# Moving the large operands of TensorE from 64 past a multiple of 512 bytes to a multiple of 512 bytes

## The chip, the core and the metric

The kernel runs on one core of one Trainium2 chip. The metric is the device time of one execution in microseconds (us); lower is better. The engines are named as the profile names them: PE is TensorE's matmul, PEld its weight load, DVE is VectorE, ACT is ScalarE, POOL is GpSimd, and SP (SyncE) issues nearly all DMAs. Each core has an on-chip memory, SBUF, of 128 partitions; an address below means a byte offset within a partition, the same in all 128. The change is about where in it tiles start. "Residue" stands for a start address modulo 512 bytes.

## The reference, cut to what matters

One decoder layer over 2048 tokens of width 1024, in float32: a gated DeltaNet mixer with 8 heads of 128, a cross-attention to 256 memory rows with 4 heads, an output projection with residual and layer norm, and a squared-ReLU MLP of width 4096 with residual and layer norm.

```python
proj = x @ w_in                                   # q, k, v, z of 8 heads, gates, memory queries
qkv = silu(causal_depthwise_conv(qkv, conv_w))    # width 4
q, k = l2_normalize(q), l2_normalize(k)
o = chunk_gated_delta_rule(q, k, v, g, beta)      # per chunk a triangular inverse, then a state update
o = rms_norm(o, gate_norm_w) * silu(z)
m = memory_attention(mq, mem_k, mem_v)
x = layer_norm(ALPHA * x + concat([o, m]) @ w_out, ln1_g, ln1_b)
x = layer_norm(ALPHA * x + square(relu(x @ w_ff1)) @ w_ff2, ln2_g, ln2_b)
```

## The kernel before

The 2048 tokens go in four blocks of 512 (`for b in range(NB)`, line 1111). Each block runs the same stages: the input projections and the DeltaNet heads, the memory attention, the output projection, and the MLP.

**Precision by threes.** A large float32 product is made of three matmuls of the type fp32r: each operand is split into a high part (a cast on ACT) and a low part (a subtraction on DVE) by `split` (line 450), and `mm3` (line 468) issues high by high, high by low and low by high. Weights arrive by DMA in `wraw` tiles and are split into `whl` tiles, 1024 columns of high and 1024 of low. The activations of the block lie in `Thi` and `Tlo`. For one block this makes 36 column groups of `w_in` times 8 times 3 = 864 such matmuls, 288 for the output projection, 768 for the first MLP product and 672 for the second: 2592 a block and 10368 in all, 512 columns wide but for some of the first MLP product, which are done in two halves of 256. The second MLP product (`ff_seven`, line 991) is a seven-product scheme; its stationary operands are the tiles `xh` and `xl`, and two of the high ones lie in the tile `kq0` under the name `hq`.

**The heads.** `dense(t)` (line 673) projects q, k, v and z of head t. For q, k and v, ACT copies the result into a `raw` tile with three halo columns ahead of it, and DVE adds the four taps from it into `cq`, `ck`, `cv`. q and k are then split into the tiles `kq0` and `kq1`. PE transposes k and then q into one PSUM bank (`ptk`, then `ptq`; the bank is `ga0` or `ga1` by the parity of the head). From the transposed k, ACT makes four squares with a running sum (`jk`: the square itself goes to a scrap tile `jk`, only the sum in `ss` is used) and four scaled copies `kd`; from the transposed q four squares `jq`. POOL turns the sums into `rk` and `bh`. `gdn_a(t)` (line 818) multiplies k by k and q (`pkq`), scales by `bh` into `dl`, inverts the triangular matrix (`invert`, beginning with the copies `Lq`), and transposes v (`ptv`). `gdn_b(t)` (line 869) walks four chunks in order (`R`, `vt`, the state), makes four squares of the result with their sums (`joss` is the scrap tile), normalizes, transposes and writes the head's output `cat`. The loop at line 1127 calls, for step t, `gdn_b(t-2)`, `gdn_a(t-1)` and `dense(t)`, in this order. The memory attention comes in the last steps; the output projection is then taken in three parts (line 1176): heads 0 to 3, the memory heads, heads 4 to 7.

**The planner.** None of this is issued in program order. Every instruction is recorded by the class `Recorder`, and its method `issue` (line 220) lays them out by list scheduling with estimated durations: an instruction earlier in the program goes first among those that are ready. A tile has a tag with a number of buffers. `place` and `ahead` (lines 237 to 259) give the buffers of a tag out strictly in program order of the tiles' first uses: with one buffer, the next tile of the tag can be taken only when every earlier tile of that tag has had it and given it back. `jk`, `jq` and `joss` are three tags (the tag is the tile's name, line 387) with one buffer each. The planner's costs depend on shapes alone, not on addresses. The engines then run the instructions in the planned order.

**Where tiles lie.** Pools lie one behind the other in the order of lines 369 to 375, each tile rounded up to 32 bytes. By the sizes in the code, `cst` ends at residue 64, so `wraw`, `whl` (pool `wp`), the 4 KB token tiles, `Thi` and `Tlo` (pool `tp`) start at residue 64. The two `raw` tiles of 515 floats take 2080 bytes each, 4160 together, so `kq0` and `kq1` behind them lie at residue 128. The 112 floats of the pool `pad` (line 372) bring the pool `sp`, with `xh`, `xl`, `ch`, `cl` and the head's tiles, back to residue 64.

Of the kernel before, what the change touches and what calls it, by code (L numbers as in the profile page):

```python
# [8 lines left out]
F32 = mybir.dt.float32  # L9
# [5 lines left out]
P = 128  # L15
TB = 512
# [320 lines left out]
def hybrid_layer(  # L337
# [24 lines left out]
    nc = tc.nc  # L362
# [6 lines left out]
    cst = ctx.enter_context(tc.tile_pool(name="cst", bufs=1))  # L369
    wp = ctx.enter_context(tc.tile_pool(name="wp", bufs=1))  # L370
    tp = ctx.enter_context(tc.tile_pool(name="tp", bufs=1))
    pad = ctx.enter_context(tc.tile_pool(name="pad", bufs=1))
    nc.vector.memset(pad.tile([P, 112], F32, name="shift"), 0.0)
    sp = ctx.enter_context(tc.tile_pool(name="sp", bufs=1))
    sm = ctx.enter_context(tc.tile_pool(name="sm", bufs=1))
    ps = ctx.enter_context(tc.tile_pool(name="ps", bufs=1, space=bass.MemoryType.PSUM))
# [6 lines left out]
    def slot(name, tag="s0", dt=F32, shape=(P, TB)):  # L383
        return rec.buf(sp, shape, dt, tag, BUFS[tag], name)

    def small(name, shape, bufs=3, dt=F32):
        return rec.buf(sm, shape, dt, name, bufs, name)

    def bank(name, tag):
        return rec.buf(ps, (P, TB), F32, tag, PBUFS[tag], name)  # L390
# [2 lines left out]
        return ap.rearrange("p (c f) -> p c f", c=NC)  # L393


    ident = cst.tile([P, P], F32, name="ident")
    make_identity(nc, ident)
    ones = cst.tile([P, P], F32, name="ones")
# [31 lines left out]
    rec = Recorder(nc, tc)  # L430
    BN_DIM = nc.vector.BN_STATS_DIM
    nc = rec
# [17 lines left out]
    def split(src, hi, lo, eng=None):  # L450
        nc.scalar.copy(out=hi, in_=src)
        (eng or nc.vector).tensor_tensor(out=lo, in0=src, in1=hi.bitcast(F32), op=ALU.subtract)
# [28 lines left out]
    def load_in(b, u):  # L481

        if b == 0:
            rt = rec.buf(wp, (P, 1024), F32, "wraw", NR, "wraw")
            nc.sync.dma_start(out=rt, in_=w_in[u])
            t, hi, lo = hilo(rt)
            nc.sync.dma_start(out=wsc[u], in_=t.bitcast(F32))
        else:
            t, hi, lo = pair()
            nc.sync.dma_start(out=t.bitcast(F32), in_=wsc[u])  # L490
        return as_cols(hi, lo)
# [33 lines left out]
    def tok_tile(name):  # L525
        return rec.buf(tp, (P, D), F32, "tok", 8, name)
# [14 lines left out]
    def project(o, w, T, n=TB, t0=0):  # L541
        for k in range(KT):
            kk = [100 * k + t for t in range(t0 // P, (t0 + n) // P)]
            mm3(o, w[0][k], w[1][k], T[0][:, k, t0:t0 + n].part(*kk), T[1][:, k, t0:t0 + n].part(*kk),
                k == 0, k == KT - 1)
# [127 lines left out]
    def dense(b, h, T, G, w0=None):  # L673
        res = {}
        for nm, o in (("q", QO), ("k", KO), ("v", VO), ("z", ZO)):
            w = w0 if w0 and nm == "q" else load_in(b, o // P + h)
            a = bank("a" + nm, "acc")
            project(a, w, T)
            c = slot("c" + nm, "d")
            th = slot("th", "th")  # L680
            if nm == "z":
                nc.scalar.activation(th, a, AF.Tanh, scale=0.5)
                nc.vector.scalar_tensor_tensor(out=c, in0=th, scalar=1.0, in1=a, op0=ALU.add, op1=ALU.mult)
            else:
                gi = o // P + h
                raw = rec.buf(tp, (P, TB + 3), F32, "raw", 2, "raw")
                nc.scalar.copy(out=raw[:, 3:], in_=a)
                nc.gpsimd.tensor_copy(raw[:, 0:3], halo[:, gi].part(gi))
                if b < NB - 1:
                    nc.gpsimd.tensor_copy(halo[:, gi].part(gi), raw[:, TB:TB + 3])  # L690
                nc.scalar.activation(c, a, AF.Copy, scale=cw[:, 72 + gi:73 + gi])
                for j in range(3):
                    nc.vector.scalar_tensor_tensor(out=c, in0=raw[:, j:j + TB], scalar=cw[:, j * 24 + gi:j * 24 + gi + 1],
                                                   in1=c, op0=ALU.mult, op1=ALU.add)
                nc.scalar.activation(th, c, AF.Tanh, scale=0.5)
                nc.vector.scalar_tensor_tensor(out=c, in0=th, scalar=1.0, in1=c, op0=ALU.add, op1=ALU.mult)
            res[nm] = c
            if nm in "qk":
                if "kq" not in res:
                    res["kq"] = [rec.buf(tp, (P, 2, TB), F32R, "kq%d" % u, 1, "kq") for u in range(2)]  # L700
                i = "kq".index(nm)
                split(c, res["kq"][0][:, i].part(i), res["kq"][1][:, i].part(i), KQE)
        par = "ga%d" % (h % 2)
        ss = small("ss", [P, 2 * NC])
        kd = res["kd"] = slot("kd", "s%d" % (h % 2))
        for n, nm in enumerate("kq"):
            pt = bank("pt" + nm, par)
            for c in range(NC):
                nc.tensor.transpose(pt[:, c * P:(c + 1) * P], res[nm][:, c * P:(c + 1) * P], ident)
            for c in range(NC):  # L710
                j = small("j" + nm, [P, P], 1)
                nc.scalar.activation(j, pt[:, c * P:(c + 1) * P], AF.Square,
                                     accum_out=ss[:, n * NC + c:n * NC + c + 1])
            if nm == "k":
                for c in range(NC):
                    nc.scalar.activation(kd[:, c * P:(c + 1) * P], pt[:, c * P:(c + 1) * P], AF.Copy,
                                         scale=G["ekd"][:, h, c:c + 1])
        nc.gpsimd.tensor_scalar_add(ss, ss, 4 * RMS_EPS)
        rk = small("rk", [P, NC])
        nc.gpsimd.tensor_tensor(out=rk, in0=ss[:, :NC], in1=mhalf, op=ALU.pow)  # L720
        res["e4"] = small("e4", [P, NC], 4)
        nc.gpsimd.tensor_scalar_mul(res["e4"], ss[:, NC:], P * RMS_EPS)
        res["vbs"] = small("vbs", [P, NC])
        nc.gpsimd.tensor_tensor(out=res["vbs"], in0=G["betah"][:, h], in1=rk, op=ALU.mult)
        bh = res["bh"] = small("bh", [P, NC])
        nc.gpsimd.tensor_tensor(out=bh, in0=G["beta"][:, h], in1=rk, op=ALU.mult)
        nc.gpsimd.tensor_tensor(out=bh, in0=bh, in1=rk, op=ALU.mult)
        res["nbe"] = small("nbe", [P, NC], 4)
        nc.gpsimd.tensor_tensor(out=res["nbe"], in0=bh, in1=G["neg"][:, h], op=ALU.mult)
        return res  # L730

    def invert(L, par):
# [14 lines left out]
        nc.vector.tensor_copy(Xc, i16.unsqueeze(2).to_broadcast([P, 16, NC]))  # L747
        B = small("Bc", [P, 16, NC], 2)
        for j in range(15):
            w = j + 1  # L750
            nc.vector.stream_shuffle(B[:, :w], Xc[:, :w], [j] * 16 + [16 + j] * 16)
            nc.vector.tensor_tensor(out=B[:, :w], in0=B[:, :w],
                                    in1=Lc[:, j:j + 1].to_broadcast([P, w, NC]), op=ALU.mult)
            nc.vector.tensor_tensor(out=Xc[:, :w], in0=Xc[:, :w], in1=B[:, :w], op=ALU.subtract)
        Z = small("Z32", [P, NC, 32], 2)
# [54 lines left out]
    def sumsq(p3, nm):  # L810
        o = small(nm, [P, NC])
        for c in range(NC):
            j = small("j" + nm, [P, P], 1)
            nc.scalar.activation(j, p3[:, c], AF.Square, accum_out=o[:, c:c + 1])
        return o

# [52 lines left out]
    def gdn_b(h, A, G, cat):  # L869
# [5 lines left out]
        for c in range(NC):  # L875
# [11 lines left out]
            nc.vector.scalar_tensor_tensor(out=Sh, in0=Sh, scalar=sc("el", c), in1=pc[:, 2 * P:3 * P],  # L887
                                           op0=ALU.mult, op1=ALU.add)
        oss = sumsq(po, "oss")
        m4 = small("m4", [P, NC])  # L890
        nc.gpsimd.tensor_scalar_mul(m4, oss, 1.0 / P)
# [79 lines left out]
    def keep_sums(u, j):  # L971

        if j == 0:
            B = [t[:, n * TB:(n + 1) * TB].part(n) for t in (tok_tile("wq"), tok_tile("wq")) for n in range(2)]
        else:
            B = [rec.buf(tp, (P, TB + 3), F32, "raw", 2, "wq")[:, :TB] for _ in range(2)]
            kq = rec.buf(tp, (P, 2, TB), F32, "kq1", 1, "wq")
            B += [kq[:, n].part(n) for n in range(2)]
        for n in range(4):
            nc.sync.dma_start(out=B[n], in_=w_ff2[u + 2 * (n // 2), n % 2][:, j * TB:(j + 1) * TB])  # L980
        for i, o, x, y in ((1, 0, 1, 0), (3, 1, 3, 1), (2, 3, 3, 0), (4, 2, 2, 3)):
            nc.vector.tensor_tensor(out=B[o], in0=B[x], in1=B[y], op=ALU.subtract)
            nc.sync.dma_start(out=tsc[u, i][:, j * TB:(j + 1) * TB].part(j), in_=B[o])
# [7 lines left out]
    def ff_seven(b, ff1_tiles, relu2, add, norm2):  # L991
        Q = 2 * P
        for g in range(NS):
# [3 lines left out]
            for v in range(2):  # L997
# [6 lines left out]
                for part in ((0, 1, 2, 3),) if g == 0 and v == 0 else ((0,), (1,), (2,), (3,)):  # L1004
                    if b == 0:
                        for j in range(2):
                            if 2 * j in part:
                                keep_sums(u0 + v, j)
# [260 lines left out]
```

## Time and profile before

| what | us |
|---|---|
| median of 3 runs (2996.95 to 2998.56) | 2997.76 |
| the profiled execution, its own time | 2999.08 |
| its span, first to last instruction | 2997.4 |

The profile is a page for one execution and a trace of it that can be asked for views: groups of instructions, waits, the chain of work that ended last, a timeline, and the busy time in given stretches. A row of the timeline gives the start in us, the duration in us, engine, line, operation, output and inputs by the program's names, shape, and a count where equal instructions follow each other. All recorded operations have line 320, that of the recorder's helper, so they are told apart by their tiles. A matmul's duration includes a modelled tail that overlaps the next one; the step from one start to the next is what PE's time is made of. A float32 matmul (not fp32r) shows as two records, a transpose as one.

Each of the four blocks repeats its pattern: block 1 has its heads from about 784 us to 1142 us, its output projection to about 1183 us and its MLP to about 1517 us.

### The profile page before, as it was taken

The numbers are of one execution on the slowest core, as the hardware profiler recorded it, in microseconds if no ns is written. First come the engines' busy times: TensorE is split into PE (matmuls) and PEld (weight loads), VectorE is DVE, ScalarE is ACT, GpSimd is POOL, SyncE is SP. The second block draws the span as 40 slices with busy tenths as digits, with TensorE's granted clock in tenths as the row PEclk, the third lists the DMA queues.
The fourth block names the chain that finished last, engine by engine and source line by source line (L and its number), as shares of the span: only waits on it lengthen the run. The fifth ranks groups of instructions, "written<-read, shape, count | busy, mean of one in ns | idle before, by whom it ended". The sixth has DMA issues, their size and how long they took to land.

```text
span 2997.4 us, 43880 instructions
## 1 busy us (share of the span) xinstructions
PE 2945.4 (98%) x15300; PEld 2428.1 (81%) x15300; DVE 2168.6 (72%) x5537; ACT 1520.3 (51%) x3582; POOL 332.4 (11%) x808
## 2 busy tenths in 40 slices
PE   7999999999999999999999999999999999999998
PEld 6888788888788878888878887888878888788886
DVE  6898977666777787655577887665667787675667
ACT  5676534544355562544445665344554556444443
POOL 1222100000112211000012221000001222000000
PEclk9999999999999999999999999999999999999999
DMA  6765566656733223444473332244446332324443
GB/s 231 253 218 180 196 209 224 200 183 192 268 142 132 106 89 102 145 137 133 151 268 130 121 119 92 87 152 144 145 159 250 126 134 96 99 88 146 143 147 134
DMA packets 127709, 469.85 MB, mean 157 GB/s; under 512 B 14464, under 2 KB 16896, under 8 KB 109056
## 3 DMA queue, kind: packets, MB, share of 16 engines
q1 hardware_dynamic: 126912, 467.00, 46.2%
q8 instruction: 120, 1.97, 0.3%
q14 instruction: 101, 0.83, 0.1%
q10 hardware_dynamic: 576, 0.06, 0.0%
HBM read 402.97 MB, written 64.03 MB: 156 GB/s over the span
## 4 chain that ended last, share of the span: by engine, by line
PE 88%; DVE 8%; ACT 2%; issue 1%; DMA 1%; POOL 0%; POOLq 0%; ACTq 0%; DVEq 0%; SPq 0%
PE af L320 42%; PE ao L320 8%; PE aq L320 6%; PE ak L320 5%; PE az L320 5%; PE av L320 4%; PE amq L320 3%; PE pc L320 3%; PE pp L320 2%; PE pq L320 2%; PE po L320 2%; PE pkq L320 1%; DVE y L320 1%; PE sps L320 1%; DVE ck L320 1%
## 5 line engine op out<-in xcount | busy, mean ns | idle before, releaser
L320 DVE TENSOR_TENSOR whl<-wraw,whl 128x1024 fp32r<-128x1024 f32 (+1 forms) x446 | 538.7, 1216 | 392.8 <-ACT whl L320 386.1
L320 PE MATMUL af<-Thi,whl 128*128 128x512 f32 (+1 forms) x2304 | 655.9, 369 | 6.9 <-DVE whl L320 4.0
L320 ACT CAST whl<-wraw 128x1024 fp32r<-128x1024 f32 (+1 forms) x446 | 466.1, 1045 | 381.8 <-PE af L320 169.0
L320 PEld LDWEIGHTS af<-Thi,whl 128*128 128x128 f32 x2304 | 421.7, 191 | 78.5 <-DVE whl L320 4.8
L320 PE MATMUL af<-whl,xh 128*128 128x512 f32 x1536 | 476.4, 391 | 3.6 <-DVE whl L320 3.6
L320 PE MATMUL af<-Tlo,whl 128*128 128x512 f32 (+1 forms) x1152 | 424.8, 369 | 0.0
L320 PE MATMUL af<-whl,xl 128*128 128x512 f32 x896 | 347.3, 390 | 0.0
L320 PEld LDWEIGHTS af<-whl,xh 128*128 128x128 f32 x1536 | 288.6, 188 | 68.6 <-DVE whl L320 6.7
L320 PE MATMUL ao<-whl,ch 128*128 128x512 f32 x768 | 249.4, 399 | 0.5 <-DVE y L320 0.5
L320 PEld LDWEIGHTS af<-Tlo,whl 128*128 128x128 f32 x1152 | 220.4, 191 | 34.8
L320 ACT ACTIVATE rl<-af 128x512 f32<-128x512 f32 x128 | 76.5, 598 | 271.0 <-PE af L320 269.0
L320 DVE SCALAR_TENSOR_TENSOR y<-y,af 128x512 f32<-128x512 f32 x224 | 151.3, 684 | 84.1 <-PE af L320 82.9
L320 PEld LDWEIGHTS af<-whl,xl 128*128 128x128 f32 x896 | 168.5, 188 | 35.5
L320 POOL TENSOR_SCALAR ve<-mv 128x1 f32<-128x1 f32 x34 | 23.3, 684 | 1528.8 <-DVE mv L320 1528.8
L320 PE MATMUL aq<-Thi,whl 128*128 128x512 f32 x512 | 181.6, 414 | 7.5 <-ACT Thi L320 7.5
L320 PE MATMUL av<-Thi,whl 128*128 128x512 f32 x512 | 173.0, 402 | 0.0
L320 PE MATMUL ak<-Thi,whl 128*128 128x512 f32 x512 | 172.9, 401 | 0.0
L320 PE MATMUL az<-Thi,whl 128*128 128x512 f32 x512 | 170.2, 400 | 0.0
L320 PEld LDWEIGHTS ao<-whl,ch 128*128 128x128 f32 x768 | 142.6, 188 | 27.0 <-DVE y L320 0.7
L320 PE MATMUL ao<-whl,cl 128*128 128x512 f32 x384 | 153.5, 400 | 0.0
L320 PEld LDWEIGHTS aq<-Thi,whl 128*128 128x128 f32 x512 | 94.3, 192 | 21.5 <-ACT Thi L320 7.5
L320 PEld LDWEIGHTS az<-Thi,whl 128*128 128x128 f32 x512 | 95.9, 190 | 18.8 <-DVE whl L320 0.5
(252 smaller groups left out, 5756.3 us busy)
## 6 DMA issues: line engine op xcount, KB each, us to landing
wraw<-in_w_ff_dram SPq DMA_DIRECT2D x224, 512.0 KB, 4.0
whl<-wsc SPq DMA_DIRECT2D x108, 1024.0 KB, 4.8
wraw<-tsc SPq DMA_DIRECT2D x128, 512.0 KB, 3.3
wsc<-whl SPq DMA_DIRECT2D x36, 1024.0 KB, 4.9
wraw<-in_w_out_dram SPq DMA_DIRECT2D x48, 512.0 KB, 4.1
wraw<-in_w_in_dram SPq DMA_DIRECT2D x35, 512.0 KB, 5.8
wq<-in_w_ff_dram SPq DMA_DIRECT2D x64, 256.0 KB, 4.3
tsc<-wq SPq DMA_DIRECT2D x64, 256.0 KB, 3.3
```

What stands on the lines that cost most here:

```text
L320: o.fn(*[res(a) for a in o.args], **{k: res(v) for k, v in o.kw.items()})
```

## The change

It does four things. It takes away the pool `pad` with its 448 bytes between `tp` and `sp`, and puts a tile of the same size, `edge`, at the front of `cst`, ahead of everything else. It widens the `raw` tiles (and the two tiles that borrow their buffers in `keep_sums`) by 56 floats, so that two of them take 4608 bytes, nine times 512. The copy into `raw` gets an explicit end, so it writes the same 512 columns. And the three scrap tiles `jk`, `jq` and `joss` become one tag `j` with one buffer, which gives 1024 bytes back.

By the sizes, all that lies behind `edge` moves up by 448 bytes, which is the same as 64 down modulo 512: `wraw`, `whl`, the token tiles, `Thi`, `Tlo` and all of `sp` go from residue 64 to 0. `kq0` and `kq1` go from 128 to 0.

```diff
-    pad = ctx.enter_context(tc.tile_pool(name="pad", bufs=1))
-    nc.vector.memset(pad.tile([P, 112], F32, name="shift"), 0.0)
...
+    edge = cst.tile([P, 112], F32, name="edge")
+    nc.vector.memset(edge, 0.0)
     ident = cst.tile([P, P], F32, name="ident")
...
-                raw = rec.buf(tp, (P, TB + 3), F32, "raw", 2, "raw")
-                nc.scalar.copy(out=raw[:, 3:], in_=a)
+                raw = rec.buf(tp, (P, TB + 3 + 56), F32, "raw", 2, "raw")
+                nc.scalar.copy(out=raw[:, 3:TB + 3], in_=a)
...
-                j = small("j" + nm, [P, P], 1)
+                j = small("j", [P, P], 1)
                 nc.scalar.activation(j, pt[:, c * P:(c + 1) * P], AF.Square,
                                      accum_out=ss[:, n * NC + c:n * NC + c + 1])
...
     def sumsq(p3, nm):
         o = small(nm, [P, NC])
         for c in range(NC):
-            j = small("j" + nm, [P, P], 1)
+            j = small("j", [P, P], 1)
             nc.scalar.activation(j, p3[:, c], AF.Square, accum_out=o[:, c:c + 1])
...
-            B = [rec.buf(tp, (P, TB + 3), F32, "raw", 2, "wq")[:, :TB] for _ in range(2)]
+            B = [rec.buf(tp, (P, TB + 3 + 56), F32, "raw", 2, "wq")[:, :TB] for _ in range(2)]
```

## The prediction

> **What bounds the kernel now.** I read the page's busy times and its chain first, then the busy time by stretches, then the timeline of the places that the change touches.
>
> ```profile
> span 2997.4 us, 43880 instructions
> PE 2945.4 (98%) x15300; PEld 2428.1 (81%) x15300; DVE 2168.6 (72%) x5537; ACT 1520.3 (51%) x3582; POOL 332.4 (11%) x808
> PE 88%; DVE 8%; ACT 2%; issue 1%; DMA 1%; POOL 0%; POOLq 0%; ACTq 0%; DVEq 0%; SPq 0%
> ```
>
> PE is busy 98% of the span, and 88% of the chain that ended last is PE. So two things can move the time: the step from one large matmul to the next, and any hole in which PE has nothing ready. Two stretches of the second block, its heads and most of its MLP (first column the stretch, then its length, then busy us by engine, granted clock, DMA share):
>
> ```profile
> 784.00:1142.00 358.00, 354.31 (x2046) 289.43 (x2045) 277.25 (x1006) 196.78 (x644) 70.17 (x188) 1.00 0.40 140
> 1200.00:1500.00 300.00, 299.49 (x1364) 248.29 (x1363) 182.39 (x257) 150.67 (x209) 0.00 (x0) 1.00 0.45 142
> ```
>
> In the MLP PE stands still for 0.5 us of 300. In the heads it stands still for 3.7 us of 358, although DVE is busy for 277 there: PE always finds another matmul, but not by much.
>
> **Part one of the change: residues.** The diff moves everything behind `edge` by 448 bytes. The distance between two operands modulo 512 is therefore what it was, with one exception: `kq0` and `kq1` stood 64 past the others and now stand with them. So there are two questions: what does it cost that operands differ in residue, and does the common residue, 64 or 0, matter by itself?
>
> The trace shows the first. In the second MLP product, `hq` lies in `kq0` (128) and all else at 64. Rows of 2 and of 1 matmul alternate; I show the starts of every third matmul:
>
> ```profile
> 1509.57 0.63 PE L320 MATMUL af<-whl,hq 128*128 128x512 f32 x2
> ...
> 1510.26 0.63 PE L320 MATMUL af<-whl,xh 128*128 128x512 f32 x2
> ...
> 1510.96 0.62 PE L320 MATMUL af<-whl,hq 128*128 128x512 f32 x2
> ...
> 1511.65 0.63 PE L320 MATMUL af<-whl,xh 128*128 128x512 f32 x2
> ...
> 1512.34 0.61 PE L320 MATMUL af<-whl,xh 128*128 128x512 f32 x2
> ...
> 1513.02 0.61 PE L320 MATMUL af<-whl,xh 128*128 128x512 f32 x2
> ...
> 1513.70 0.62 PE L320 MATMUL af<-whl,xh 128*128 128x512 f32 x2
> ```
>
> Three matmuls take 0.69, 0.70, 0.69, 0.69 us around the two uses of `hq`, then 0.68 and 0.68: 227 ns each. Each such pair of uses loses 0.05 us against four times 0.68.
>
> ```profile
> L320 PE MATMUL af<-whl,hq 128*128 128x512 f32 x256 | 80.1, 394 | 0.0
> L320 PE MATMUL pkq<-kq 128*128 128x256 f32 x384 | 64.4, 294 | 1.2 <-ACT jq L320 1.2
> ```
>
> 256 matmuls with `hq` are 64 such places: 64 x 0.05 = **3 us gained**. The 384 `pkq` have both operands in `kq` and keep their distance: 0.
>
> The Trainium skill speaks against this term: "TensorE: Matmul & The Clock Gate", section "Step-by-step: what each phase is for", says that the moving operand and the weight load have two independent ports into SBUF, and that loading the next weights takes nothing from the running matmul. By that rule the term is 0 and the sum below 3 us higher; the steps of 0.69 and 0.70 us speak against it.
>
> For the common residue I have no row with two values, so I bound it. The step isn't all arithmetic, as a stretch at half the granted clock shows (first two rows: length, busy times, clock 0.50 and 1.00):
>
> ```profile
> 453.50:456.30 2.80, 2.80 (x15) 2.80 (x14) 2.80 (x6) 0.00 (x0) 1.21 (x2) 0.50 0.91 282
> 459.00:462.00 3.00, 3.00 (x28) 3.00 (x27) 2.55 (x4) 0.59 (x1) 0.00 (x0) 1.00 0.45 164
> ...
> 454.66 0.63 PE L320 MATMUL af<-Thi,whl 128*128 128x256 f32 x2
> ...
> 455.30 0.63 PE L320 MATMUL af<-Thi,whl 128*128 128x256 f32 x2
> ...
> 459.44 0.40 PE L320 MATMUL af<-Thi,whl 128*128 128x256 f32 x2
> ...
> 459.79 0.40 PE L320 MATMUL af<-Thi,whl 128*128 128x256 f32 x2
> ```
>
> At half clock three matmuls of 256 columns take 0.64 us, 213 ns each. At full clock that would be 107; they take 0.35 to 0.36, about 118 to 120. So some 13 ns per matmul don't shrink with the clock; for 512 columns likewise 227 instead of 213. If a common residue of 0 removed them, 10368 matmuls would save up to 138 us; if it made every step like the disturbed ones near `hq` (0.693 / 3 = 231 ns), it would cost 10368 x 4 ns = 41 us. I take 0, since the nearest row is the steady 0.68 itself: what disturbs it in the trace is a difference of residues, and the differences stay. Both ends are kept as rivals.
>
> The Trainium skill, same page, section "Back-to-back issue gap", gives N/2.4 + 2.5 ns as the step, 216 ns for 512 columns. The trace has 227, so by that rule 11 ns of the step need an explanation, and alignment could be it: 10368 x 11 = 114 us, an estimate from that page.
>
> The `memset` is the same, moved. DVE reads `raw` at three starts 4 bytes apart already, so I cost its new start at nothing. DMAs land at other residues; PE's stretch above at a DMA share of 0.45 waits 0.5 us in 300 for anything, so that hides them.
>
> **Part two: one scrap tile in place of three.** This isn't a matter of addresses, but it binds the planner. The single buffer of `j` is given out in program order: `joss` of head t-2, then `jk` and `jq` of head t. See what the order is now, at heads 1 and 3 of the second block (`joss`, `R` and the row at 918.76 are head 1's; the rest is head 3's):
>
> ```profile
> 904.06 0.60 PE L320 MATMUL ptk<-ident,ck 128*128 128x128 f32 x4
> 905.09 0.27 ACT L320 ACTIVATE jk<-ptk 128x128 f32<-128x128 f32 x1
> ...
> 908.78 0.28 ACT L320 ACTIVATE jq<-ptq 128x128 f32<-128x128 f32 x1
> ...
> 911.06 1.04 POOL L320 TENSOR_TENSOR rk<-ss,mhalf 128x4 f32<-128x4 f32 x1
> ...
> 914.49 0.35 DVE L320 SCALAR_TENSOR_TENSOR R<-pc,nbe,vb 128x128 f32<-128x128 f32 x1
> 914.84 0.69 DVE L320 TENSOR_TENSOR dl<-gb,m_l 128x512 f32<-128x512 f32 x1
> ...
> 918.46 0.34 DVE L320 SCALAR_TENSOR_TENSOR dl<-pkq,bh,dl 128x128 f32<-128x128 f32 x1
> ...
> 918.76 0.23 ACT L320 ACTIVATION_READ_ACCUMULATOR joss<-po 128x1 f32 x1
> ...
> 926.84 0.26 DVE L320 COPY Lq<-dl 32x128 f32<-32x128 f32 x1
> ```
>
> Head 3 makes its squares from 905 us, 14 us ahead of head 1's last `joss` (918.99). Afterwards they must follow it. Behind the squares stand `ptq` (same bank as `ptk`), `jq`, POOL's `rk` and `bh`, then `dl` and the inverse. Part of the delay is covered: `dl` waits anyway for a slot that head 1's last `R` frees (914.49, then 914.84). What the squares-to-inverse run takes when nothing else holds it is seen at heads 1 and 5:
>
> ```profile
> 839.89 0.27 ACT L320 ACTIVATE jk<-ptk 128x128 f32<-128x128 f32 x1
> ...
> 852.65 0.28 DVE L320 COPY Lq<-dl 32x128 f32<-32x128 f32 x1
> ...
> 979.08 0.26 ACT L320 ACTIVATE jk<-ptk 128x128 f32<-128x128 f32 x1
> ...
> 994.00 0.27 DVE L320 COPY Lq<-dl 32x128 f32<-32x128 f32 x1
> ```
>
> 12.8 to 14.9 us. So head 3's inverse starts at 918.99 + 12.8 to 14.9 = 931.8 to 933.9 instead of 926.84: 5 to 7 us late. For head 4:
>
> ```profile
> 966.85 0.21 ACT L320 ACTIVATION_READ_ACCUMULATOR joss<-po 128x1 f32 x1
> ...
> 972.05 0.28 DVE L320 COPY Lq<-dl 32x128 f32<-32x128 f32 x1
> ```
>
> 967.06 + 12.8 to 14.9 = 979.9 to 982.0, 8 to 10 us late. Heads of one parity follow each other on one PSUM bank, so 2 delays (heads 3 and 5) or 3 (2, 4, 6) add up: from 2 x 5 to 3 x 10, 10 to 30 us per block in the head chains. What PE does meanwhile decides. At the end of the stage it has work in hand (matmuls of the output projection alone, tile `ao`, before and after 1141.7 us; then the last head's `cat`):
>
> ```profile
> 794.00:1141.70 347.70, 31.29 (x114) 19.93 (x115) 6.13 (x9) 1.00 0.38 134
> 1141.70:1197.00 55.30, 40.89 (x176) 32.52 (x174) 10.27 (x15) 0.97 0.27 83
> 1140.88 0.74 DVE L320 SCALAR_TENSOR_TENSOR cat<-pto,gnwh,cz 128x512 f32<-128x512 f32 x1
> ```
>
> When the last head's `cat` is there, 176 matmuls of the output projection are left; 96 need heads 4 to 7, the other 80 x 0.227 = 18 us don't, and can fill a late end. In the middle of the stage there is less: the projections of the next heads wait for the 11 buffers that late heads still hold, and the memory attention comes only from step 6 on. Bounds per block: 0 if PE always finds other work, 30 if the chain sets the end with no cover. The nearest row is the stage's 3.7 us of idle PE, so I take a value near the low end: one uncovered wait of about 3 us a block, 4 x 3 = **12 us lost**.
>
> **The sum.** -3 + 12 + 0 = +9 us: the profiled execution from 2999.08 to 3008, and on the median, which is 1.3 us lower, 2997.76 to **3007**. A measurement of this kernel can tell about 0.2%, 6 us, from no change.
>
> **The rivals.**
> - *Covered (not slower).* PE fills every hole that the squares make, from the projections still open and the 18 us above. Then only the 3 us of `hq` are left: 2995. For it: 3.7 us idle in 358. It decides if no stretch of the heads gains idle PE.
> - *The common residue counts (faster).* The 13 ns go. In the heads DVE, at 277 of 358 us, stands behind PE, so I count only the 1728 large matmuls a block outside the 864 projections: 4 x 1728 x 13 ns = 90 us, with the 9 above 2917; up to 138, 2869. For it: those ns don't scale with the clock. Against: a difference in residue, not the residue, is what the trace shows at work.
> - *The head chain takes over (slower).* The 10 to 30 us a block are covered by little: at 10 a block, 3035 with the `hq` gain.
> - *Residue 0 is worse.* 231 ns at every step: +41, about 3048.
> - *It does not do what it says.* If tiles are rounded otherwise than to 32 bytes, `kq` stays apart and 3 us are missing; that changes little.
>
> **How the numbers follow.** Forecast, a few uncovered us (2999 to 3020): 0.38, of which 0.13 lie within 6 us of before. Covered: 0.22, of which 0.04 lie below 2992. Residue counts: 0.17. Chain takes over: 0.17. Residue 0 worse: 0.06. Faster: 0.17 + 0.04 = 0.21; the same: 0.18 + 0.13 = 0.31; slower: 0.25 + 0.17 + 0.06 = 0.48. The range 2988 to 3055 leaves out the 0.17 below and a little above.
>
> **What would show it.** In the timeline of the changed kernel: `jk` of head t behind `joss` of head t-2; `Lq` of heads 2 to 6 some 5 to 10 us further behind the block's start; idle PE between 784 and 1142 grown from 3.7 us to about 7; three matmuls around `hq` in 0.68 us; all other steps still 0.68. I am wrong if those steps are 0.64 or 0.69, or if the heads take no more time.

## The result, and the profile after

| | us |
|---|---|
| before, median of 6 runs (2996.14 to 2999.76) | 2997.94 |
| after, median of 6 runs (3013.97 to 3017.76) | 3016.86 |
| ratio, 95% interval | 1.0061 (1.0049 to 1.0074) |
| the profiled execution after, its own time; its span | 3017.72; 3016.0 |

The change makes the kernel 18.9 us slower; the forecast was 9 us slower. The page of the changed kernel, its busy times and the shares of its chain:

```profile
span 3016.0 us, 43968 instructions
PE 2951.9 (98%) x15300; PEld 2428.4 (81%) x15300; DVE 2164.9 (72%) x5537; ACT 1514.5 (50%) x3582; POOL 334.3 (11%) x808
PE 85%; DVE 8%; ACT 4%; POOL 2%; issue 1%; DMA 1%; ACTq 0%; POOLq 0%; DVEq 0%; SPq 0%
```

The instructions of PE are the same 15300, but ACT and POOL together rose from 2% to 6% of the chain that ended last: something small on ACT and POOL now sets the end somewhere. That is not what a change of addresses would do to the steps of PE.

**The steps around `hq`.** The timeline of PE in the second MLP product, as in the prediction's part one (rows of one `xl` matmul between them are left out):

```profile
1525.56 0.62 PE L320 MATMUL af<-whl,hq 128*128 128x512 f32 x2
...
1526.24 0.62 PE L320 MATMUL af<-whl,xh 128*128 128x512 f32 x2
...
1526.92 0.62 PE L320 MATMUL af<-whl,hq 128*128 128x512 f32 x2
...
1527.60 0.62 PE L320 MATMUL af<-whl,xh 128*128 128x512 f32 x2
...
1528.28 0.62 PE L320 MATMUL af<-whl,xh 128*128 128x512 f32 x2
```

Every three matmuls take 0.68 us, around `hq` as elsewhere. Summed in each trace over the steps from one 512-column matmul to the next (those up to 260 ns), the excess over about 226.7 ns falls from 11.3 us to 7.4 us: 3.8 us gained, 3.4 of them within ten matmuls of an `hq`. The rest of the steps is as it was, at residue 0 as at 64.

**The order of the squares.** The timeline of the changed kernel at heads 0 and 2 of the second block (`j<-po` is head 0's `joss`, `j<-ptk` head 2's `jk`):

```profile
896.90 0.63 PE L320 MATMUL ptk<-ident,ck 128*128 128x128 f32 x4
897.61 0.35 ACT L320 ACTIVATE kd<-ptk,ekd 128x128 f32<-128x128 f32 x1
...
910.92 0.31 ACT L320 ACTIVATE j<-po 128x128 f32<-128x128 f32 x1
911.08 0.24 ACT L320 ACTIVATION_READ_ACCUMULATOR j<-po 128x1 f32 x1
911.42 0.33 ACT L320 ACTIVATE j<-ptk 128x128 f32<-128x128 f32 x1
...
914.15 0.60 PE L320 MATMUL ptq<-ident,cq 128*128 128x128 f32 x4
```

Head 2's k stands transposed in PSUM from 897.5 us, and ACT makes the copies `kd` of it at once. The squares of the same bank wait until 911.42, right behind the last `joss` of head 0. `ptq`, which needs the bank, comes 17 us after `ptk`. (In the kernel before even `jq`, which reads `ptq`, stands only 4.7 us behind `ptk`, by the prediction's rows of head 3.)

What that does to the inverse of head 6, and to the blocks, is seen in the first `aq` matmul of blocks 1, 2 and 3 and the first `Lq` of that head. Before:

```profile
783.66 0.40 PE L320 MATMUL aq<-Thi,whl 128*128 128x512 f32 x1
...
1042.24 0.31 DVE L320 COPY Lq<-dl 32x128 f32<-32x128 f32 x1
...
1517.56 0.39 PE L320 MATMUL aq<-Thi,whl 128*128 128x512 f32 x1
...
2251.65 0.39 PE L320 MATMUL aq<-Thi,whl 128*128 128x512 f32 x1
```

After:

```profile
797.06 0.39 PE L320 MATMUL aq<-Thi,whl 128*128 128x512 f32 x1
...
1074.54 0.26 DVE L320 COPY Lq<-dl 32x128 f32<-32x128 f32 x1
...
1533.49 0.39 PE L320 MATMUL aq<-Thi,whl 128*128 128x512 f32 x1
...
2268.41 0.39 PE L320 MATMUL aq<-Thi,whl 128*128 128x512 f32 x1
```

Head 6's inverse starts 277.5 us behind its block's start where it was 258.6: 19 us late. But block 1 lasts 736.4 us against 733.9 and block 2 734.9 against 734.1, so almost all of those 19 us is filled with other work. **Block 0 is where the time went**: block 1 begins 13.4 us later.

**Why block 0.** Busy time in the stretch from the last `amq` matmul, with which a block's projections end, to the last `cat`, blocks 0 and 1 (stretch, length, PE, PEld, DVE, ACT, POOL, granted clock, DMA share, GB/s). Before:

```profile
350.00:404.70 54.70, 52.95 (x299) 41.57 (x298) 44.61 (x122) 27.31 (x83) 4.17 (x6) 1.00 0.67 225
1096.90:1141.60 44.70, 44.58 (x252) 35.08 (x252) 30.14 (x71) 23.16 (x67) 4.13 (x6) 1.00 0.36 119
```

After:

```profile
342.60:420.40 77.80, 71.17 (x394) 54.36 (x393) 60.68 (x202) 34.91 (x112) 9.28 (x19) 0.93 0.54 180
1097.60:1159.20 61.60, 59.75 (x360) 46.57 (x359) 47.08 (x160) 31.10 (x95) 5.60 (x12) 1.00 0.30 94
```

With the heads late, PE takes the projections earlier (in block 1 they end 300.5 us behind the block's start instead of 313.2), so that what is left behind them grows, by 17 us in block 1 and by 23 us in block 0. Block 1 had this stretch full, 0.1 us idle in 44.7, and now waits 1.9 us. Block 0 already waited 1.8 us before: it had no cover left. Now it waits 6.6 us, and its mean clock is 0.93. Where that comes from (stretches of the changed kernel, and the longest wait in them):

```profile
347.30:350.70 3.40, 2.23 (x12) 1.46 (x10) 2.42 (x11) 1.52 (x7) 2.83 (x7) 1.00 0.33 78
350.70:354.10 3.40, 1.80 (x14) 1.64 (x14) 3.40 (x15) 1.29 (x5) 0.19 (x1) 1.00 0.26 88
354.20:364.40 10.20, 9.73 (x43) 6.58 (x44) 7.29 (x33) 4.45 (x14) 2.18 (x6) 0.50 0.34 118
```

```profile
351.93 0.95 PE L320 MATMUL pkq<-kq 128*128 128x256 f32 x6 [1.93 <-DVE dl L320]
```

`pkq` of head 7 waits 1.93 us for a `dl`, in the run of steps from the late squares to the inverse. PE is busy for 4.0 of 6.8 us, and then its granted clock is 0.50 for 10.2 us. PE is busy for 9.7 us of these; at full clock at most half of that would go, so the dip costs up to 4.9 us (an estimate from this row). With the 4.9 us of added waiting that accounts for up to 10 of the 13.4 us; the rest was not followed.

### The profile page after: what moved, and what is told of

It is laid out like the page before. It is cut to its first block, busy times and chain, and to the rows that moved or that the text cites. A ratio compares the mean times of both kernels' runs of the same rounds, so it can differ in the third digit from the quotient of the medians.

```text
span 3016.0 us, 43968 instructions
## 1 busy us (share of the span) xinstructions
PE 2951.9 (98%) x15300; PEld 2428.4 (81%) x15300; DVE 2164.9 (72%) x5537; ACT 1514.5 (50%) x3582; POOL 334.3 (11%) x808
## 4 chain that ended last, share of the span: by engine, by line
PE 85%; DVE 8%; ACT 4%; POOL 2%; issue 1%; DMA 1%; ACTq 0%; POOLq 0%; DVEq 0%; SPq 0%
PE af L320 41%; PE ao L320 8%; PE ak L320 6%; PE aq L320 4%; PE az L320 4%; PE av L320 4%; PE pc L320 3%; PE amq L320 2%; PE pp L320 2%; PE pq L320 2%; PE po L320 2%; DVE y L320 1%; PE pkq L320 1%; ACT j L320 1%; DVE whl L320 1%
## 5 line engine op out<-in xcount | busy, mean ns | idle before, releaser
L320 POOL TENSOR_SCALAR ve<-mv 128x1 f32<-128x1 f32 x34 | 21.5, 634 | 1519.4 <-DVE mv L320 1519.4
```

The costliest lines, as they stand in the source:

```text
L320: o.fn(*[res(a) for a in o.args], **{k: res(v) for k, v in o.kw.items()})
```

## The experiments

Theory 1: the order that the single tag `j` gives costs all of the loss, the moved `hq` gains 3 to 4 us, and the common residue does nothing. Theory 2, the rival: the residue 0 itself costs, outside the large steps. Each time below is a median, beside the median of the kernel before on the same chip.

### `joss` on its own tag again (joss_own)

Edit of the changed kernel, in `sumsq`:

```diff
-            j = small("j", [P, P], 1)
+            j = small("joss", [P, P], 1)
```

> The changed kernel, with joss on a tag of its own again (jk and jq still share one). All residues stay at 0. Theory 1, the order given by the single tag costs everything and the common residue nothing: the loss of 18.9 us goes and the gain around hq (3.8 us by the steps of the two traces) is left, 2998 - 4 = 2994. Theory 2, the residue 0 itself costs, somewhere outside the steps of the large matmuls: no change against the changed kernel, 3017.

2994.73 beside 2997.35; ratio 0.9990 (0.9981 to 0.9999). The loss is gone and a little is gained. Heads run as before: here is head 2 of the second block,

```profile
881.86 0.63 PE L320 MATMUL ptk<-ident,ck 128*128 128x128 f32 x4
882.57 0.26 ACT L320 ACTIVATE j<-ptk 128x128 f32<-128x128 f32 x1
...
889.29 0.60 PE L320 MATMUL ptq<-ident,cq 128*128 128x128 f32 x4
```

with the squares 0.7 us behind the transposes' start and `ptq` at 7 us in place of 17. Theory 2 falls: all operands stand at 0 here.

### The order alone (order_alone)

Edit of the kernel before, in `dense` and in `sumsq`:

```diff
-                j = small("j" + nm, [P, P], 1)
+                j = small("j", [P, P], 1)
...
-            j = small("j" + nm, [P, P], 1)
+            j = small("j", [P, P], 1)
```

> The kernel before, all residues as they were, with jk, jq and joss on one tag of one buffer. Theory 1: the whole loss and no gain, 2998 + 19 + 4 = 3021. Theory 2: 2998. If order and residue cost half each: about 3008.

3019.13 beside 2997.35; ratio 1.0070 (1.0057 to 1.0083): 21.8 us lost. By the starts of the blocks in its trace, 14.9 us fall in block 0 and 1.5, 1.5 and 1.4 in the others, 19.3 in all, as the spans differ (3016.7 against 2997.4).

The last three are not the price of the order alone, because the clock differs too. In the kernel before, PE's granted clock is 0.50 for some 3.4 us behind the output projection of each of blocks 1, 2 and 3; in this trace it stays at 1.00 there, behind the same waits. Here is the place in block 1, first in the kernel before, then in this one (two stretches each, the one ahead and the one in question):

```profile
1187.20:1190.60 3.40, 1.85 (x14) 1.44 (x13) 3.40 (x6) 0.99 (x2) 0.71 (x1) 1.00 0.00 0
1190.70:1194.00 3.30, 3.30 (x18) 3.30 (x17) 3.30 (x6) 0.00 (x0) 1.20 (x2) 0.50 0.85 273
...
1205.60:1209.00 3.40, 1.84 (x13) 1.55 (x13) 3.40 (x6) 0.58 (x1) 1.08 (x1) 1.00 0.20 18
1209.10:1212.40 3.30, 3.30 (x30) 3.30 (x30) 3.30 (x5) 0.34 (x1) 0.89 (x1) 1.00 0.77 290
```

PE gets through 18 matmuls in 3.3 us in the one and 30 in the other. So blocks 1 to 3 of this trace are helped by the clock, and the order costs more there than 1.5 us; the two kernels with the shared order in some blocks only, below, show how much.

### `kq0` and `kq1` alone moved to 64 (kq_alone)

Edit of the kernel before, no order changed:

```diff
-    pad = ctx.enter_context(tc.tile_pool(name="pad", bufs=1))
-    nc.vector.memset(pad.tile([P, 112], F32, name="shift"), 0.0)
...
-                raw = rec.buf(tp, (P, TB + 3), F32, "raw", 2, "raw")
-                nc.scalar.copy(out=raw[:, 3:], in_=a)
+                raw = rec.buf(tp, (P, TB + 3 + 56), F32, "raw", 2, "raw")
+                nc.scalar.copy(out=raw[:, 3:TB + 3], in_=a)
```

> The kernel before with raw widened by 56 floats and the pad dropped: kq0 and kq1 go from 128 to 64, so that all large operands stand at 64, and no order changes. If only the difference between residues costs: the 64 places around hq go from 0.69 and 0.70 us to 0.68, 2998 - 4 = 2994, the same as with all at 0 and joss on its own tag. If residue 0 is better than 64 by itself: this one stays above that one. If hq's residue is not what disturbs the steps: 2998.

2996.03 beside 2997.35; ratio 0.9995 (0.9986 to 1.0003). The time alone can't tell this from no change. The steps can: behind `hq` they take 226.9 ns in place of 231.9, and their total excess falls by 3.3 us (11.3 to 8.0). The steps are those of the kernel with all at 0 (table below).

### All of `sp` at 128 (sp_at_128)

Edit of the kernel before: only the two lines of `pad` are taken out.

> The kernel before without the pad: all of the pool sp goes to 128, where kq0 and kq1 stand already, while whl stays at 64. So in the output projection and the second MLP product every stationary operand now differs from the moving one by 64, and none differs from its neighbours. If a difference between stationary and moving operand costs: each of these 4 x (288 + 672) = 3840 steps takes 231 ns or more in place of 227, 3840 x 4 = 15 us more, about 3013. If only a change from one stationary operand to the next costs: nothing is lost and hq's disturbance goes too, 2994.

3012.06 beside 2997.35; ratio 1.0049 (1.0037 to 1.0062). A constant difference costs at every step. Output projection of the second block in this trace, rows of two:

```profile
1159.97 0.63 PE L320 MATMUL ao<-whl,ch 128*128 128x512 f32 x2
...
1160.67 0.63 PE L320 MATMUL ao<-whl,ch 128*128 128x512 f32 x2
...
1161.38 0.63 PE L320 MATMUL ao<-whl,ch 128*128 128x512 f32 x2
...
1162.07 0.63 PE L320 MATMUL ao<-whl,ch 128*128 128x512 f32 x2
```

Three of them take 0.70, 0.71 and 0.69 us. The steps are 231 and 236 ns in about equal numbers. The steps with `Thi` or `Tlo` as the moving operand, which did not move, stay at 227.8 ns. Summed, the excess of all large steps is 30.7 us against 11.3, 19 us more, and the time rose by 14.7 (11 to 19 by the interval). The clock would account for the difference: this trace, too, lacks the three stretches at clock 0.50 behind the output projections of blocks 1 to 3, each worth some 1.5 us (next section).

### Which block pays (shared_block0, shared_blocks123)

Edit of the changed kernel; the second kernel has `not (b > 0)` in place of `not (b == 0)`:

```diff
-    def sumsq(p3, nm):
+    def sumsq(p3, nm, own):
...
-            j = small("j", [P, P], 1)
+            j = small("joss" if own else "j", [P, P], 1)
...
-                gdn_b(t - 2, A.pop(t - 2), G, cat[t - 2])
+                gdn_b(t - 2, A.pop(t - 2), G, cat[t - 2], not (b == 0))
```

> The changed kernel with joss on the shared tag in block 0 only; in blocks 1 to 3 it has its own. By the starts of the blocks in the two traces (changed kernel against joss on its own tag: block 1 begins 14.5 us later, block 2 another 3, block 3 another 2, the end another 5), block 0 carries most of the loss: 2994.7 + 14.5 = 3009. If the order costs the same in every block: a quarter of the 22 us, 3000.

> The complement: joss on the shared tag in blocks 1 to 3, on its own in block 0. If block 0 carries most: 2994.7 + 22.1 - 14.5 = 3002. If every block pays the same: three quarters of the 22 us, 3011.

Shared in block 0 alone: 3007.18 beside 2998.66; ratio 1.0031 (1.0020 to 1.0043). Shared in blocks 1 to 3: 3002.36 beside the same; ratio 1.0015 (1.0007 to 1.0024). Against the kernel with `joss` on its own tag, which is 2.6 us under its before, that is 11 us in the one block and 6 in the other three together. In the first of the two the granted clock drops to 0.50 between 355 and 370 us, as in the changed kernel; in the second it stays at 1.00 there. The 11 and the 6 us are 4 short of the 21.5 us between the changed kernel and the one with `joss` on its own tag; the intervals, some 3 us each way, leave room for that.

The two traces compare blocks 1 to 3 with the shared order and without it at the same clock. In both, block 1 has one stretch of 3.4 us at clock 0.50 behind its output projection and block 2 has none. From one block's first `aq` matmul to the next one's, block 1 takes 736.5 us with the shared order and 733.3 us without, block 2 takes 734.9 and 731.8 us, and block 3 (one such stretch in both), to the end, 747.6 and 745.0 us: the order costs about 3 us in each. Not quite half of it is idle PE (7.6 us against 6.2 in block 1); the rest was not followed. Blocks 1 and 2 of the kernel without the shared order there differ by 1.5 us (733.3 and 731.8), which is what one such stretch at half clock costs, since in the kernel before, where both have one, they differ by 0.2 us.

### Two buffers for the one tag (two_buffers)

```diff
-                j = small("j", [P, P], 1)
+                j = small("j", [P, P], 2)
...
-            j = small("j", [P, P], 1)
+            j = small("j", [P, P], 2)
```

> The changed kernel with two buffers for the tag j in place of one. Theory A, the strict order of handing out binds and not the space: jk of head t can start at most one tile ahead of joss of head t-2, about 0.5 us earlier, so nearly all of the loss stays: 3015. Theory B, the single buffer is too little space: the loss is halved or gone, 2995 to 3006.

3014.25 beside 2998.66; ratio 1.0054 (1.0042 to 1.0067). Twice the space leaves 15.6 of the 18.9 us. With one buffer or two it is the order in which the tag is given out that binds. By the code of `ahead`, the first `jk` of head t can pass the four `joss` of head t-2 only with five buffers or more; that was not run.

### One plain tile that the planner doesn't know (plain_scrap)

The kernel with `kq0` and `kq1` at 64 (above), and the squares write a tile that isn't one of the planner's buffers:

```diff
+    junk = cst.tile([P, P], F32, name="junk")
...
-                j = small("j" + nm, [P, P], 1)
-                nc.scalar.activation(j, pt[:, c * P:(c + 1) * P], AF.Square,
+                nc.scalar.activation(junk, pt[:, c * P:(c + 1) * P], AF.Square,
...
-            j = small("j" + nm, [P, P], 1)
-            nc.scalar.activation(j, p3[:, c], AF.Square, accum_out=o[:, c:c + 1])
+            nc.scalar.activation(junk, p3[:, c], AF.Square, accum_out=o[:, c:c + 1])
```

> All at residue 64 (raw widened, no pad, as in the run with kq0 and kq1 moved alone), and the squares of jk, jq and joss go to one plain tile that the planner doesn't know, so that it hands nothing out and orders nothing. It gives 1024 bytes back as the change does. If the order given by the tag is the cost and not the one tile as such: 2995, like three tags. If the three kinds of squares disturb each other when they write the same place: up to 3017.

2995.26 beside 2998.66; ratio 0.9989 (0.9980 to 0.9998). All three kinds of squares write one place, as in the change, and nothing is lost. So the shared place costs nothing here; the order that the tag imposed did.

### Which differences count (diff_32, diff_128, diff_256, residue_96)

To the kernel with the plain tile a pad is added ahead of `sp`; here for 32 bytes, then with 32 and 64 floats for 128 and 256:

```diff
+    pad = ctx.enter_context(tc.tile_pool(name="pad", bufs=1))
+    nc.vector.memset(pad.tile([P, 8], F32, name="shift"), 0.0)
     sp = ctx.enter_context(tc.tile_pool(name="sp", bufs=1))
```

The fourth is the kernel with `joss` on its own tag, with an edge of 8 floats:

```diff
-    edge = cst.tile([P, 112], F32, name="edge")
+    edge = cst.tile([P, 8], F32, name="edge")
```

> The kernel with the plain scrap tile (2995.3), with 32 bytes of pad ahead of the pool sp: xh, xl, ch and cl stand at 96, whl and hq at 64. If any difference between the stationary and the moving operand costs as 64 did (steps of 231 and 236 in turn, 14.7 us): 3007 to 3010. If only a whole 64 bytes counts: 2995, steps of 227.

> The same with 256 bytes of pad: xh, xl, ch and cl at 320, whl and hq at 64. If any difference costs alike: 3007 to 3010, steps of 231 and 236. If the cost goes with the size of the difference: more than 3010. If only small differences disturb: 2995.

> The changed kernel with joss on its own tag (2994.7), with an edge of 8 floats in place of 112: all large operands stand at 96 in place of 0. If only differences between operands count and the common residue doesn't: 2995, steps of 227. If a start that is no multiple of 64 costs by itself: steps above 227 in all 10368 matmuls, at 4 ns each 41 us, 3036.

> As the runs with 32 and 256 bytes of pad, with 128: xh, xl, ch and cl at 192, whl and hq at 64. If the disturbance follows the start modulo 128: 2995, steps of 227. If it follows the start modulo 256 (or 512 with 256 as a harmless case): 3009 to 3013, steps of 231 to 236.

The steps are worked out from each trace: from one 512-column matmul to the next, `xh` or `xl` as the first of the two, those up to 260 ns.

| kernel | `whl` | `xh`, `xl` | `hq` | mean step, ns | us, beside before | ratio (95%) |
|---|---|---|---|---|---|---|
| before | 64 | 64 | 128 | 227.6 | 2997.94 | |
| after | 0 | 0 | 0 | 226.8 | 3016.86 / 2997.94 | 1.0061 (1.0049 to 1.0074) |
| kq_alone | 64 | 64 | 64 | 226.9 | 2996.03 / 2997.35 | 0.9995 (0.9986 to 1.0003) |
| residue_96 | 96 | 96 | 96 | 226.9 | 2994.00 / 2997.67 | 0.9989 (0.9979 to 0.9999) |
| diff_32 | 64 | 96 | 64 | 233.3 | 3013.07 / 2997.67 | 1.0049 (1.0034 to 1.0064) |
| sp_at_128 | 64 | 128 | 128 | 233.3 | 3012.06 / 2997.35 | 1.0049 (1.0037 to 1.0062) |
| diff_128 | 64 | 192 | 64 | 232.8 | 3012.36 / 2999.48 | 1.0045 (1.0031 to 1.0059) |
| diff_256 | 64 | 320 | 64 | 226.9 | 2995.20 / 2997.67 | 0.9991 (0.9981 to 1.0) |

The timeline of the output projection with a difference of 256, beside which the rows of the difference of 64 above may be laid:

```profile
1159.00 0.62 PE L320 MATMUL ao<-whl,ch 128*128 128x512 f32 x2
...
1159.68 0.62 PE L320 MATMUL ao<-whl,ch 128*128 128x512 f32 x2
...
1160.36 0.62 PE L320 MATMUL ao<-whl,ch 128*128 128x512 f32 x2
...
1161.04 0.62 PE L320 MATMUL ao<-whl,ch 128*128 128x512 f32 x2
```

0.68 us for three, undisturbed. Differences of 32, 64 and 128 cost alike, 256 costs nothing, and a common start that is no multiple of 64 costs nothing. The kernel with 32 bytes came out 3 us above the 3007 to 3010 that were expected of it.

## Why the prediction came out as it did

**The `hq` term (3 us gained): right.** 0.69 and 0.70 us became 0.68, and the steps lost 3.8 us in all where 3 were counted (the disturbance runs on for some matmuls behind each place). Five kernels that have this gain and not the order lie 1.3 to 3.7 us under before. The rule of the Trainium skill that was set against the term ("TensorE: Matmul & The Clock Gate", section "Step-by-step: what each phase is for", two independent ports) would have the step independent of where the weights lie; in these runs it depends on how the starts of the two operands stand to each other, 233 against 227 ns. Whether the ports are what they meet at, no run shows.

**The common residue (0): right.** The steady step is 227 ns at 0, 64 and 96. Both rivals on this point fall, the one in which 13 ns a matmul go and the one in which every step takes 231. The 11 ns above the N/2.4 + 2.5 of the Trainium skill ("TensorE: Matmul & The Clock Gate", section "Back-to-back issue gap", which gives it for isolated matmuls) are there at each of the three, so the common start isn't their cause. What is, stays open.

**The order of `j` (12 us lost): the mechanism was right, the size was not.** This is the step of the sum that failed: "one uncovered wait of about 3 us a block, 4 x 3 = 12 us lost". It measured 21.8 us (order_alone). For blocks 1 to 3 the term was right in size: 3.2, 3.1 and 2.6 us at equal clock (shared_blocks123 against shared_block0), and 6 us in all three by the medians. That the 3 us hit is in part luck, since idle PE, from which they were taken, makes not quite half of them. For block 0 the term was four to five times too low: 11 us by the medians, 14.9 us in the trace of order_alone. The value for every block was taken from block 1, where PE was busy throughout the stretch behind the projections; block 0 stood apart already in the profile before (52.95 of 54.70 us busy there, against 44.58 of 44.70), and the prediction did not look at it. The step also left out the clock. In block 0 the granted clock fell to 0.50 for 10 us or more in all four kernels with the shared order there, and at that place in none of the other ten. That the waits bring it is argued from these traces and the rows above; no run held the waits alone.

**The signs.** `jk` of head t behind `joss` of head t-2: seen. `Lq` of heads 2 to 6 later by 5 to 10 us: by their first rows, against the block's start, 5, 6, 16, 14 and 19 us in block 1, so the delays add up along a parity as the prediction's upper bound had it, and heads 4 to 6 lie beyond the 5 to 10 us of the sign. Idle PE from 784 to 1142 us, 3.7 to about 7: the stretch of the changed kernel is

```profile
784.00:1142.00 358.00, 352.53 (x2017) 286.04 (x2016) 277.75 (x1012) 193.20 (x632) 75.16 (x189) 1.00 0.41 143
```

5.5 us, though the block now begins 13 us later in it. The other steps still 0.68 us: seen.

**The rivals.** "Covered" fell: block 0 loses 11 to 15 us, the others about 3 us each, and their heads gain idle PE. "The head chain takes over" fell as put, with 10 to 30 us in each block; the loss of block 0 alone, at 11 to 15, is of that size. That tiles might be rounded otherwise fell with the steps at `hq`.

**Beating both.** The kernel with `joss` on its own tag keeps every residue of the change and runs in 2994.73 (0.9990 of before, 0.9981 to 0.9999); with all at 64 and the plain scrap tile it is 2995.26. Either is about 3 us better than before and 22 better than the change.

## What to carry to other kernels

A scratch tile whose content nobody reads is not free when a planner gives its buffer out in program order: it then orders the work that writes it, and a second buffer hardly helped; take it out of the planner's hands or give it a tag for each stage. Work out the cover of a delay for every block, above all for the first one, from a stretch that begins where the filling work ends. Before a loss is read off the lengths of blocks, see whether the granted clock was the same in both. For addresses, what counted here is that stationary and moving operand of a large fp32r matmul start at the same place or 256 bytes apart, and not 32, 64 or 128 apart; the common value (0, 64 or 96) did not matter.

## What the runs showed of the hardware that was not expected

- The disturbance between operands is gone at a difference of 256 bytes, so it does not follow the start modulo 512: 232.8 to 233.3 ns a step with differences of 32, 64 and 128, 226.9 with 256. It may go by the start modulo 256, but no other values were tried. At 64 the steps come as 231 and 236 ns in about equal numbers. Which part of the chip this is, no run shows.
- The granted clock fell to 0.50 for 10.2 us though PE's longest wait there was 1.93 us; PE had been busy for 2.23 and 1.80 of 3.4 us in the two stretches ahead. Between 350 and 370 us it shows in all four profiles with the shared order in block 0 (the changed kernel, order_alone, shared_block0, two_buffers) and in none of the other ten. A wait need not bring a dip: behind the output projection of block 1 PE was busy for 1.85 of 3.4 us in the kernel before and for 1.84 in order_alone, and the clock fell to 0.50 in the first and stayed at 1.00 in the second. The Trainium skill ("TensorE: Matmul & The Clock Gate", section "HAM oscillation — how this bites in real kernels") puts the rule as no idle gaps of PE above some 3.4 us; here a dip came behind several shorter ones. What the dip costs by itself, up to 4.9 us by its busy row, was not tried on its own.
